# The norm of a feed-forward input moved behind the expanding product, onto GpSimd

## The chip, the cores and the metric

The kernel runs on one core of a Trainium2 chip, as one launch. The metric is the device time of that launch in microseconds (us). A core has a matrix engine (TensorE, in the rows PE, with its weight loads as PEld), two elementwise engines (VectorE, DVE, and ScalarE, ACT), a third, slower one (GpSimd, POOL) and a queue that issues DMAs (SyncE, SP). Each engine takes its instructions in order, and semaphores make one wait for another. Matrix products land in PSUM, which has eight banks of 128 x 512 numbers here; all else lives in SBUF.

## The reference

Two transformer blocks over 256 tokens of 2048 numbers. The first (two layers with three kinds of attention) and the mixer and memory attention of the second are not touched. The change lies in the last part of the second block:

```
h = rmsnorm(x, pre_norm_ffn)             # x * rsqrt(mean(x*x) + eps) * gain, per token
hid = h @ w_up                           # 2048 -> 2 * 5632
hid = causal convolution of width 3 over the tokens, per column, + bias
gate, up = split(hid)
x = x + rmsnorm((gelu(gate) * up) @ w_down, post_norm_ffn)
```

The norm factor rsqrt(...) is one number per token. It can be multiplied into h, or after the product into each row (token) of hid, but ahead of the convolution, which mixes tokens.

## The kernel before, in words

All products are done in split form: a 32-bit number is written as hi + lo, hi rounded to the matrix engine's format, and hi*hi + hi*lo + lo*hi are added up. Each 128 x 512 piece of a weight (**raw**) is brought in by a DMA from the SP queue (two pieces each, three buffers); ACT makes its **hi** by a copy (L431), DVE its **lo** by a subtraction raw - hi (L432). There are four hi and four lo buffers, so the split can run at most a few pieces ahead of the product that reads them.

The last part is `ffn`. Its input X (8 tiles, 2 x 128 tokens by 4 x 512 columns) is made by `close` of the attention before it: DVE and POOL add the attention's result to X (L1592, L1590), ACT sums the squares of the new X (L1597), DVE adds them up (L1601). `normT` then builds the transposed, normed, split input in 8 units of two 128-column pieces. For one unit, `unit` transposes four 128 x 128 tiles of X on PE into a PSUM bank (L566, tile trs, two banks), multiplies on DVE by the gain (a column vector) and the row of norms rb (L576), copies to hi on ACT (L583) and subtracts on DVE (L584). The row rb comes from the sums: DVE scales them (L409), POOL takes the power -1/2 (L410), two small PE products spread the two columns of 128 norms over all partitions (L599, tile rbt), and DVE copies that to SBUF (L607). Unit 0 cannot be scaled before rb is there.

The expanding product is 22 **blocks** of `denseT2`. A block makes four 128 x 256 results (two gate and two up column groups), each in its own PSUM bank (tiles upd, upd and ups, ups or upt, upo in turn), over 16 steps of 128 input columns (kt 0 to 15). A step takes one hi and one lo weight piece and does eight products (L539: weight hi by [h hi, h lo], 512 columns; L540: weight lo by h hi, 256 columns). Then `evac` empties the four banks. For each result: ACT copies the half with h lo to a tile **us** (L2012), DVE adds the other half from PSUM (L2013), ACT multiplies by the last convolution tap and adds the bias, into cv (L2014), and DVE adds the two shifted taps (L2015, L2017). After these come the gelu on ACT (L2019), the product gate * up on DVE (L2020) and the split of the result (L431, L432). The next block's products run on PE at the same time, into other banks, and its weight splits stand between these instructions on ACT and DVE. Three buffers serve the us tiles.

The order of the instructions on each engine is set by a scheduler from the code; it interleaves the evacuation of one block with the weight splits of the next. The contracting product (`dense`, w_down) follows, and at the end `post` with `close` adds the normed result to X and writes it out. `post` also fetches four rows of gains by DMAs from the POOL queue (L1557) for the contraction's evacuation.

Of the kernel before, what the change touches and what calls it, by code (L numbers as in the profile page):

```python
# [13 lines left out]
OP = mybir.AluOpType  # L14
# [4 lines left out]
D = 2048  # L19
# [1530 lines left out]
class Block2(Block1):  # L1550
# [447 lines left out]

    def ffn(self, X, ss, out):
        nc, a = self.nc, self.a  # L2000
        h = self.normT(X, self.gain("pre_ffn"), ss=ss, both=True)
        units = []
        for b in range(22):
            def evac(banks):
                c = {}
                for g in range(2):
                    c[g] = self.B("cv", bufs=4)
                    for i in range(2):
                        ct = g * 44 + 2 * b + i
                        p, d = banks[2 * g + i], c[g][:, i * 256:i * 256 + 256]  # L2010
                        s = self.temp("us")[:, :256]
                        nc.scalar.activation(s, p[:, 256:], AF.Copy)  # L2012
                        nc.vector.tensor_add(s, s, p[:, :256])  # L2013
                        nc.scalar.activation(d, s, AF.Identity, scale=self.v("cw2", ct), bias=self.v("cb", ct))  # L2014
                        nc.vector.scalar_tensor_tensor(d[:, 1:], s[:, :255], self.v("cw1", ct), d[:, 1:],  # L2015
                                                       op0=OP.mult, op1=OP.add)
                        nc.vector.scalar_tensor_tensor(d[:, 2:], s[:, :254], self.v("cw0", ct), d[:, 2:],  # L2017
                                                       op0=OP.mult, op1=OP.add)
                nc.scalar.activation(c[0], c[0], AF.Gelu_apprx_tanh)  # L2019
                nc.vector.tensor_mul(c[0], c[0], c[1])  # L2020
                new = (lambda name, dt: self.B(name, tag="act", bufs=16, dt=dt)) if b < 8 else None
                units.append(self.halves(c[0], new))

            self.denseT2(h, self.w("ffn_w_up_2"), [(256 * b, 256), (DFF + 256 * b, 256)], evac,
                         "ddss" if b % 2 else "ddto", what="up")
        ev, close = self.post(X, 2 * D, out)
        act = Act(256, 44, units.__getitem__)
        for j in range(4):
            self.dense(act, list(range(44)), self.w("ffn_w_down_2"), [(512 * j, 512)], [0, 1], ev(j), what="down")
        close()  # L2030
# [76 lines left out]
```

## Time and profile before

| | us |
|---|---|
| three timed runs | 3441.53, 3451.6, 3455.27 (median 3451.6) |
| the profiled execution | 3443.87, of which the span shown is 3442.1 |
| last product of the attention before | starts at 2678.57 |
| first expanding product | 2693.77 |
| last expanding product | 3184.1 |
| end of the span | 3442.1 |

The profile is one execution. Times in its rows count from the start of the span. A row of a timeline gives start, duration, engine, line, operation, output <- inputs with shapes, how many were merged into it, and in brackets how long the engine had been idle before it and what ended that. The names of tiles are those of the program without buffer numbers.

### The profile page before, as it was taken

How to read it: one execution, taken by the hardware profiler on the slowest of the kernel's cores; microseconds unless marked ns; L12 is line 12 of the kernel's file. 1: busy time of each engine (PE TensorE's matmuls, PEld its weight loads, DVE VectorE, ACT ScalarE, POOL GpSimd, SP SyncE). 2: the span in 40 equal slices, each digit the busy share in tenths (PEclk: the TensorE clock that was granted, in tenths of full speed). 3: DMA queues.
4: the chain of work that ended last, by engine and by line, in shares of the span. 5: the costliest groups of instructions: out<-in, count | busy, mean ns of one | idle time of the engine just before them, and what ended most of it. 6: DMA issues, size and time to landing. Idle time of an engine off the chain costs nothing. (4 is left out here: it accounts for less than half of the span.)

```text
span 3442.1 us, 51876 instructions
## 1 busy us (share of the span) xinstructions
PE 3323.3 (97%) x18122; PEld 2790.0 (81%) x18122; DVE 2335.5 (68%) x5073; ACT 1818.0 (53%) x3652; POOL 320.9 (9%) x472
## 2 busy tenths in 40 slices
PE   7999999999999999998999999999999899999998
PEld 4577778788788888887777999888788788888886
DVE  3478988778867575877674556555666777777554
ACT  3345655336435355765574445555555666666544
POOL 1022221103120121111110000000000000000000
PEclk9999999999999999999999999999999999999999
DMA  8845444642565544444454636666655466666665
GB/s 291 290 124 158 132 148 133 220 127 81 169 212 171 162 118 139 144 152 149 156 163 147 184 120 183 192 189 191 208 175 168 150 187 190 191 195 199 193 191 165
DMA packets 226758, 590.11 MB, mean 171 GB/s; under 512 B 39904, under 2 KB 63184, under 8 KB 226496
## 3 DMA queue, kind: packets, MB, share of 16 engines
q1 hardware_dynamic: 221104, 570.41, 53.5%
q0 software_dynamic: 4864, 15.69, 1.5%
q8 instruction: 142, 2.33, 0.3%
q14 instruction: 120, 0.98, 0.1%
q10 hardware_dynamic: 528, 0.71, 0.1%
HBM read 582.48 MB, written 4.24 MB: 170 GB/s over the span
## 5 line engine op out<-in xcount | busy, mean ns | idle before, releaser
L432 DVE TENSOR_TENSOR lo<-raw,hi 128x512 fp32r<-128x512 f32 (+3 forms) x1788 | 1200.3, 678 | 793.5 <-ACT hi L431 765.0
L431 ACT ACTIVATE hi<-raw 128x512 fp32r<-128x512 f32 (+3 forms) x1788 | 1086.9, 614 | 1180.0 <-DVE lo L432 324.2
L784 DVE SCALAR_TENSOR_TENSOR scr<-raw,cb 128x512 f32<-128x512 f32 x448 | 301.2, 698 | 31.2 <-DMA raw<-in_w_ada_dram 16.3
L410 POOL TENSOR_TENSOR sm<-sm,mhalf 128x2 f32<-128x2 f32 (+4 forms) x116 | 119.3, 1030 | 1383.8 <-DVE sm L409 1378.6
L492 PE MATMUL downd<-hi,hi 128*128 128x512 f32 x352 | 137.8, 391 | 0.0
L494 PE MATMUL downd<-hi,lo 128*128 128x512 f32 x352 | 137.7, 391 | 0.0
L493 PE MATMUL downd<-lo,hi 128*128 128x512 f32 x352 | 137.7, 391 | 0.0
L647 ACT ACTIVATE P<-Ss,sm 128x512 f32<-128x512 f32 (+1 forms) x164 | 99.4, 607 | 67.5 <-DVE sm L643 49.3
L539 PE MATMUL upd<-hi,hi 128*128 128x512 f32 x352 | 132.8, 394 | 0.0
L539 PE MATMUL upd<-lo,hi 128*128 128x512 f32 x352 | 132.1, 392 | 0.0
L419 ACT ACTIVATE PT<-pTt 128x256 f32<-128x256 f32 x226 | 79.2, 381 | 64.6 <-PE pTt L664 55.2
L492 PE MATMUL L0outd<-hi,hi 128*128 128x512 f32 x256 | 101.4, 396 | 4.3 <-DVE ot L1407 3.0
L516 PE MATMUL L0zd<-hi,lo 128*128 128x512 f32 x256 | 100.2, 392 | 2.2 <-DVE lo L432 2.1
L513 PE MATMUL L0zd<-hi,hi 128*128 128x512 f32 x256 | 100.6, 393 | 0.4 <-DVE kpe L425 0.4
L643 DVE TENSOR_REDUCE sm<-Ss 128x1 f32<-128x512 f32 (+1 forms) x164 | 95.0, 584 | 7.8 <-PE Ss L636 6.8
L494 PE MATMUL L0outd<-hi,lo 128*128 128x512 f32 x256 | 99.9, 392 | 0.3 <-DVE lo L432 0.3
L493 PE MATMUL L0outd<-lo,hi 128*128 128x512 f32 x256 | 100.1, 391 | 0.0
L515 PE MATMUL L0zd<-lo,hi 128*128 128x512 f32 x256 | 99.9, 390 | 0.0
L879 POOL CAST pad<-q 64x128 fp32r<-64x128 f32 x156 | 62.4, 407 | 401.4 <-PE Ss L636 313.0
L540 PE MATMUL upd<-hi,lo 128*128 128x256 f32 x352 | 98.9, 281 | 0.0
L540 PE MATMUL upd<-lo,lo 128*128 128x256 f32 x352 | 98.6, 281 | 0.0
L664 PE MATMUL pTt<-ident,P 128*128 128x128 f32 x536 | 87.3, 276 | 5.8 <-DVE PT L425 1.8
(616 smaller groups left out, 9374.1 us busy)
## 6 DMA issues: line engine op xcount, KB each, us to landing
raw<-in_w_in_dram SPq DMA_DIRECT2D x344, 512.0 KB, 3.7
raw<-in_w_ada_dram SPq DMA_DIRECT2D x384, 256.0 KB, 3.5
raw<-in_ffn_w_up_dram SPq DMA_DIRECT2D x176, 512.0 KB, 4.2
raw<-in_w_out_dram SPq DMA_DIRECT2D x104, 512.0 KB, 3.6
raw<-in_ffn_w_down_dram SPq DMA_DIRECT2D x88, 512.0 KB, 4.1
raw<-in_w_proj_b_dram SPq DMA_DIRECT2D x32, 512.0 KB, 4.1
raw<-in_w_in_dram SPq DMA_DIRECT2D x32, 288.0 KB, 3.3
raw<-in_w_proj_a_dram SPq DMA_DIRECT2D x16, 512.0 KB, 4.2
```

What stands on the lines that cost most here:

```text
L410: nc.gpsimd.tensor_tensor(r, ms, self.mhalf[:, :n], op=OP.pow)
L431: self.nc.scalar.activation(hi, src, AF.Copy)
L432: self.nc.vector.tensor_sub(lo, src, hi.bitcast(F32))
L492: nc.tensor.matmul(ps[t][:, a], lhsT=xh, rhs=hi[:, a], start=first, stop=False)
L493: nc.tensor.matmul(ps[t][:, a], lhsT=xh, rhs=lo[:, a], start=False, stop=False)
L494: nc.tensor.matmul(ps[t][:, a], lhsT=xl, rhs=hi[:, a], start=False, stop=last)
L513: nc.tensor.matmul(p, lhsT=hi[:, s], rhs=xh, start=kt == 0 and c % per == 0, stop=False, skip_group_check=True)
L515: nc.tensor.matmul(p, lhsT=hi[:, s], rhs=xl, start=False, stop=False, skip_group_check=True)
L516: nc.tensor.matmul(p, lhsT=lo[:, s], rhs=xh, start=False, stop=kt == nk - 1, skip_group_check=True)
L539: nc.tensor.matmul(banks[c], lhsT=hi[:, s], rhs=x, start=kt == 0, stop=False, skip_group_check=True)
L540: nc.tensor.matmul(banks[c][:, :256], lhsT=lo[:, s], rhs=x[:, :256], start=False, stop=kt == nk - 1, skip_group_check=True)
L784: nc.vector.scalar_tensor_tensor(self.temp("scr"), raw, 1.0, st[s], op0=OP.mult, op1=OP.mult, accum_out=st["p"][:, s, k, q:q + 1])
```

## The change

The units of the feed-forward input are made with `plain=True`: transposed, multiplied by the gain and split, without the row of norms. The first two units are asked for ahead of the norm's own instructions (`h.need(1)`). The row rb of norms is made once, into a tile of its own, and in `evac` POOL multiplies each us tile by it, between the addition of the two halves and the convolution.

```diff
     def ffn(self, X, ss, out):
         nc, a = self.nc, self.a
-        h = self.normT(X, self.gain("pre_ffn"), ss=ss, both=True)
+        h = self.normT(X, self.gain("pre_ffn"), both=True, plain=True)
+        h.need(1)
+        rb = self.rows([self.rstd(ss[t], 1, D) for t in range(2)], self.B("rb", bufs=1, cols=256))
         units = []
...
                         s = self.temp("us")[:, :256]
                         nc.scalar.activation(s, p[:, 256:], AF.Copy)
                         nc.vector.tensor_add(s, s, p[:, :256])
+                        nc.gpsimd.tensor_tensor(s, s, rb, op=OP.mult)
                         nc.scalar.activation(d, s, AF.Identity, scale=self.v("cw2", ct), bias=self.v("cb", ct))
```

With `plain=True`, `unit` takes its branch without rb (L574, a multiplication by the gain alone, in place of L576). Below `evac`'s new line the line numbers are three higher than before: the copy is L2014, the addition L2015, the new multiplication L2016, the tap and bias L2017, the shifted taps L2018 and L2020, the gelu L2022.

**PE where the feed-forward begins.** trs are the transposes of the units (28456 and 28468 units 0 and 1; 28533 and 28573 units 2 and 3), rbt the spread norms, upd the first expanding product. Before:

```order
L566 MATMUL trs_28491<-ident,x_4618_18303 128x128
L599 MATMUL rbt_28475<-ident,sm_28467 128x128
L599 MATMUL rbt_28475<-ident,sm_28471 128x128
L566 MATMUL trs_28533<-ident,x_4674_18516 128x128
L566 MATMUL trs_28533<-ident,x_4678_18524 128x128
```

Now:

```order
L566 MATMUL trs_28533<-ident,x_4678_18524 128x128
L566 MATMUL trs_28573<-ident,x_4674_18516 128x128
L599 MATMUL rbt_28489<-ident,sm_28481 128x128
L599 MATMUL rbt_28489<-ident,sm_28485 128x128
L539 MATMUL upd_28493<-hi_28464,hi_28381 128x512
L540 MATMUL upd_28493<-hi_28464,lo_28382 128x256
```

The spreading of the norms moved behind the transposes of units 2 and 3, and now stands directly ahead of the first expanding product.

**ACT at the evacuation of a block in the middle** (block 8 before, block 8 now; hi<-raw are the weight splits of the next block, cv the tap and bias). Before:

```order
L2012 ACTIVATE us_30990<-upd_30777 128x256
L2012 ACTIVATE us_30996<-upd_30778 128x256
L2014 ACTIVATE cv_30989<-us_30990,vt 128x256
L2012 ACTIVATE us_31003<-ups_30779 128x256
L2014 ACTIVATE cv_30989<-us_30996,vt 128x256
L431 ACTIVATE hi_31027<-raw_31025 128x512
L2014 ACTIVATE cv_31002<-us_31003,vt 128x256
L2012 ACTIVATE us_31009<-ups_30780 128x256
L431 ACTIVATE hi_31039<-raw_31025 128x512
L2019 ACTIVATE cv_30989<-cv_30989 128x512
```

Now:

```order
L2014 ACTIVATE us_31026<-upd_30813 128x256
L2014 ACTIVATE us_31033<-upd_30814 128x256
L2017 ACTIVATE cv_31025<-us_31026,vt 128x256
L2014 ACTIVATE us_31041<-ups_30815 128x256
L2017 ACTIVATE cv_31025<-us_31033,vt 128x256
L431 ACTIVATE hi_31067<-raw_31065 128x512
L431 ACTIVATE hi_31079<-raw_31065 128x512
L2017 ACTIVATE cv_31040<-us_31041,vt 128x256
L2014 ACTIVATE us_31048<-ups_30816 128x256
L431 ACTIVATE hi_31093<-raw_31091 128x512
L2022 ACTIVATE cv_31025<-cv_31025 128x512
```

One weight split moved ahead of the third tap; the first two splits still stand behind the first two taps, and each tap now waits for POOL's multiplication of its us tile.

**DVE at the same place** (lo<-raw are the weight splits). Before:

```order
L2013 TENSOR_TENSOR us_30990<-us_30990,upd_30777 128x256
L2013 TENSOR_TENSOR us_30996<-us_30996,upd_30778 128x256
L2015 SCALAR_TENSOR_TENSOR cv_30989<-us_30990,vt,cv_30989 128x255
L2013 TENSOR_TENSOR us_31003<-us_31003,ups_30779 128x256
L2017 SCALAR_TENSOR_TENSOR cv_30989<-us_30990,vt,cv_30989 128x254
L2015 SCALAR_TENSOR_TENSOR cv_30989<-us_30996,vt,cv_30989 128x255
L432 TENSOR_TENSOR lo_31028<-raw_31025,hi_31027 128x512
L2017 SCALAR_TENSOR_TENSOR cv_30989<-us_30996,vt,cv_30989 128x254
L2015 SCALAR_TENSOR_TENSOR cv_31002<-us_31003,vt,cv_31002 128x255
L2013 TENSOR_TENSOR us_31009<-us_31009,ups_30780 128x256
L2017 SCALAR_TENSOR_TENSOR cv_31002<-us_31003,vt,cv_31002 128x254
L432 TENSOR_TENSOR lo_31040<-raw_31025,hi_31039 128x512
```

Now:

```order
L2015 TENSOR_TENSOR us_31026<-us_31026,upd_30813 128x256
L2015 TENSOR_TENSOR us_31033<-us_31033,upd_30814 128x256
L2018 SCALAR_TENSOR_TENSOR cv_31025<-us_31026,vt,cv_31025 128x255
L2015 TENSOR_TENSOR us_31041<-us_31041,ups_30815 128x256
L2020 SCALAR_TENSOR_TENSOR cv_31025<-us_31026,vt,cv_31025 128x254
L2018 SCALAR_TENSOR_TENSOR cv_31025<-us_31033,vt,cv_31025 128x255
L432 TENSOR_TENSOR lo_31068<-raw_31065,hi_31067 128x512
L2020 SCALAR_TENSOR_TENSOR cv_31025<-us_31033,vt,cv_31025 128x254
L2018 SCALAR_TENSOR_TENSOR cv_31040<-us_31041,vt,cv_31040 128x255
L2015 TENSOR_TENSOR us_31048<-us_31048,ups_30816 128x256
L2020 SCALAR_TENSOR_TENSOR cv_31040<-us_31041,vt,cv_31040 128x254
L432 TENSOR_TENSOR lo_31080<-raw_31065,hi_31079 128x512
```

The first twelve stand as before. The next weight split is moved ahead of the fourth result's first shifted tap. POOL's queue, which had nothing between the norm's powers and the four DMAs of L1557, now holds 88 multiplications there, four for each block.

## Rows read from the trace of the kernel before

**Rows 1.** The page's first line.
```profile
span 3442.1 us, 51876 instructions
```

**Rows 2.** Busy time by stage: stretch, length, busy us (instructions) of each engine, TensorE's granted clock, DMA share, GB/s.
```profile
2678.00:2696.00 18.00, 7.85 (x31) 6.08 (x30) 14.43 (x31) 11.11 (x30) 6.03 (x6) 0.62 0.22 72
2696.00:3184.50 488.50, 488.50 (x2822) 430.14 (x2821) 358.26 (x666) 308.88 (x573) 2.19 (x4) 1.00 0.62 190
3184.50:3442.00 257.50, 243.11 (x1064) 199.25 (x1062) 136.05 (x206) 119.99 (x201) 4.94 (x4) 0.98 0.60 183
```

**Rows 3.** Waits from 2725 to 3180: total us, times, longest us.
```profile
PEld upd L540 <- DVE lo L432: 0.8, 3, 0.4
```

**Rows 4.** Timeline of PE where the feed-forward begins.
```profile
2689.56 1.31 PE L599 MATMUL rbt<-ident,sm 128*128 128x128 f32 x4 [4.79 <-POOL sm L410]
...
2693.77 0.78 PE L539 MATMUL upd<-hi,hi 128*128 128x512 f32 x1
...
2697.66 0.39 PE L539 MATMUL upd<-hi,hi 128*128 128x512 f32 x1
```

**Rows 5.** Timelines of ACT, POOL and DVE at the same place.
```profile
2687.92 0.61 ACT L1597 ACTIVATE sq<-x 128x512 f32<-128x512 f32 x1
...
2688.96 1.06 POOL L410 TENSOR_TENSOR sm<-sm,mhalf 128x1 f32<-128x1 f32 x2 [2.31 <-DVE sm L409]
...
2691.36 1.66 DVE L576 SCALAR_TENSOR_TENSOR h<-trs,vt,rb 128x256 f32<-128x256 f32 x4
...
2692.94 0.42 DVE L584 TENSOR_TENSOR hi<-h,hi 128x256 fp32r<-128x256 f32 x1
```

**Rows 6.** Timeline of ACT at the evacuation of block 8.
```profile
2894.94 0.39 ACT L2012 ACTIVATE us<-upd 128x256 f32<-128x256 f32 x1 [0.18 <-PE upd L540]
...
2895.91 0.59 ACT L2014 ACTIVATE cv<-us,vt 128x256 f32<-128x256 f32 x1
```

**Rows 7.** Timeline of DVE at the same evacuation.
```profile
2895.40 0.41 DVE L2013 TENSOR_TENSOR us<-us,upd 128x256 f32<-128x256 f32 x1
...
2900.17 0.68 DVE L432 TENSOR_TENSOR lo<-raw,hi 128x512 fp32r<-128x512 f32 x1
```

**Rows 8.** Timeline of weight loads, first use of the lo piece of kt 3.
```profile
2900.98 0.19 PEld L540 LDWEIGHTS upd<-lo,lo 128*128 128x128 f32 x1
```

**Rows 9.** Line L1129: duration ns min/median/max, first and last start.
```profile
L1129 POOL TENSOR_TENSOR H<-H,cs x32: 722/738/1192, 142.9 to 1277.9; 128x256 f32<-128x256 f32 x32
```

**Rows 10.** Timelines of POOL and DVE where both work on SBUF tiles.
```profile
176.49 0.77 POOL L1129 TENSOR_TENSOR H<-H,cs 128x256 f32<-128x256 f32 x1 [0.60 <-DMA H<-in_rp_dram]
...
176.59 1.23 DVE L432 TENSOR_TENSOR lo<-raw,hi 128x512 fp32r<-128x512 f32 x1
...
928.19 1.29 POOL L1410 TENSOR_TENSOR x<-xo,ot 128x512 f32<-128x512 f32 x1
...
928.62 1.42 DVE L432 TENSOR_TENSOR lo<-raw,hi 128x512 fp32r<-128x512 f32 x1 [0.75 <-ACT hi L431]
```

**Rows 11.** Timeline of PE after single idle stretches.
```profile
495.48 0.50 PE L493 MATMUL L0cqd<-lo,hi 128*128 128x512 f32 x1 [2.19 <-DVE lo L432]
495.82 0.39 PE L494 MATMUL L0cqd<-hi,lo 128*128 128x512 f32 x1
...
2576.85 0.58 PE L516 MATMUL xkd<-hi,lo 128*128 128x256 f32 x1 [3.12 <-DVE lo L432]
2577.23 0.41 PE L513 MATMUL xkd<-hi,hi 128*128 128x256 f32 x1
...
2579.99 0.28 PE L513 MATMUL xkd<-hi,hi 128*128 128x256 f32 x1
```

**Rows 12.** POOL's DMAs of gains, their landing, and DVE's first use of one.
```profile
3171.84 0.54 POOL L1557 DMA_DIRECT2D row<-in_vb_dram  x1 [0.85 <-PE ups L540]
...
row<-in_vb_dram POOLq DMA_DIRECT2D x4, 256.0 KB, 6.5
...
3245.71 0.69 DVE L1575 TENSOR_TENSOR y<-downd,row 128x512 f32<-128x512 f32 x1 [0.72 <-ACT sq L1573]
```

## The prediction

> **What bounds the kernel now.** I read the page's first line for the span, the table of busy time by stage, the waits inside the expanding product, and then timelines, engine by engine, at two places: where the feed-forward begins, and at one evacuation in the middle.
>
> The span is 3442.1 us [rows 1]. In the stretch of the expanding product, 488.5 us long, PE is busy for all 488.50 at a granted clock of 1.00, which is 2.4 GHz, while DVE works 358 us, ACT 309 and POOL 2 [rows 2]. So this stage is bound by PE; no change on another engine can shorten it, and POOL looks free. But the average hides how close DVE is. The one wait of PE's weight loads in it is on the weight split's lo: 0.8 us in three cases [rows 3]. Block 8 shows why: the lo piece of kt 3 is finished by DVE at 2900.17 + 0.68 = 2900.85 [rows 7], and its first weight load starts at 2900.98 [rows 8]. 0.13 us is all the cover there. The next block's fourth split stands on DVE behind nearly all of the evacuation, and the block is 488.5 / 22 = 22.2 us long, so what the evacuation is late by beyond 0.13 us PE loses 22 times.
>
> Where the feed-forward begins the chain is serial: in the 18 us from 2678 PE is busy for 7.85 at a mean clock of 0.62 [rows 2]. The last squares end at 2687.92 + 0.61 = 2688.53, the two powers on POOL run from 2688.96 to 2690.02 [rows 5], the spread norms end at 2689.56 + 1.31 = 2690.87, and the first expanding product starts at 2693.77 [rows 4].
>
> **Part 1: the beginning.** What stood between 2690.87 and 2693.77, 2.90 us, was the copy of rb, the multiplication of the first units (1.66 for four, from 2691.36), their copies on ACT and their subtractions on DVE (0.42 each, from 2692.94) [rows 5]. Now the transposes, the gain and the split need only X, and can be done ahead of the norms or beside them. But the spread norms stand on PE directly ahead of the first product, as the order shows, so PE still waits for the sums and the powers: the wait isn't removed, only what followed it. DVE does the four multiplications by the gain (1.66) and a subtraction (0.42) among the sums, and the second power has to wait for part of them. I put that at a quarter of their 2.08 us, 0.5, with a little for the product's own start: gain 2.90 - 0.6 = 2.3 us. Bounds: nothing (the norms become later by as much as is taken from behind them), and all 2.90. The multiplication by the gain in later units stays one instruction on DVE of about the same length: 0.
>
> **Part 2: 88 multiplications on POOL, four for each of 22 blocks.** Their own work is cheap: 128x256 of two SBUF inputs takes POOL 738 ns in the median, 722 to 1192 [rows 9], so 88 x 0.74 = 65 us in a stage of 488 in which POOL is idle. What counts is what they hold up, in two ways.
>
> First, the tap on ACT waits for POOL. In block 8 the first addition ends at 2895.40 + 0.41 = 2895.81 [rows 7] and the tap follows at 2895.91 [rows 6], a handoff of 0.10. Now the multiplication runs from 2895.91 to 2896.65 and the tap starts at 2896.75: 0.84 later. ACT is in order, and behind the first two taps stand the splits hi of the next block's kt 2 and kt 3; on DVE behind their shifted taps stand the two lo.
>
> Second, POOL and DVE do not run side by side on SBUF tiles. A split on DVE of 0.68 alone [rows 7] that was issued 0.10 behind the start of a POOL addition of 0.77 took 1.23, and one issued 0.43 behind the start of one of 1.29 took 1.42 [rows 10]. In both it ended about half a microsecond after POOL did (177.82 against 177.26; 930.04 against 929.48): it waited for POOL to end. So each multiplication costs DVE its whole length wherever DVE has a two-input SBUF instruction to do. The shifted taps and lo splits are of that kind.
>
> The sum to the lo of kt 3. The first multiplication delays everything behind it by 0.84. The second runs while ACT does the first tap (0.59) and DVE has nothing but that to wait for: 0. The third falls between the shifted taps of the first two results, the fourth directly ahead of the split of kt 3 (it follows the fourth addition, and the order on DVE has one shifted tap between that and the split): 0.74 each. Late by 0.84 + 0.74 + 0.74 = 2.32, less the cover of 0.13: 2.19 us of idle PE per block. The order also moved one hi split ahead of the third tap, which helps its ACT half, but the lo on DVE keeps its place, so I give no credit. Times 22 (the last block's evacuation lies beside the first steps of the contraction, which takes splits at nearly the same rate): 48.2 us. Once PE has stopped, the later splits have caught up by the same amount, and each block starts afresh.
>
> Bounds for a block: if POOL and DVE did not hinder each other, 0.84 - 0.13 = 0.71 us, in all 15.6; if all four multiplications came in series at the longest seen, 0.20 + 4 x 1.19 - 0.13 = 4.8, in all 106. A gain is excluded, since PE was never idle there. I take 2.19, as the rows of the same shape are at the median length when nothing precedes them on DVE.
>
> **What is hidden.** The four DMAs of gains on POOL's queue now stand behind the last multiplication. Their last was issued at 3171.84 and such a one lands in 6.5 us; DVE first needs one at 3245.71 [rows 12]. Issued some 8 us behind the end of the expanding product (3184.5 [rows 2]) they land by about 3200, still 45 us early: 0. Without that cover they would cost what they are late by. The us tiles have three buffers and are held 0.8 us longer; the fourth copy needs the first one's buffer, whose shifted taps stand before it on DVE anyhow: 0.
>
> **Sum.** The profiled execution took 3443.87 with its 3442.1 of span. 3443.9 - 2.3 + 48.2 = 3489.8; I forecast 3490. The median of the three runs, 3451.6, lies 7.7 above the profiled execution and would give 3497; the range takes that in.
>
> **Rivals.**
> 1. Not slower: the evacuation hides the multiplications. It has the next block's 22 us to finish in, and a hi split was moved forward. Then POOL and DVE would have to take turns in DVE's pauses, so that kt 3's lo is late by no more than its cover; from 0.9 us per block (17 + 2.3, over 22) the kernel is measurably slower. Against it: 0.13 us of cover, and the 1.23 and 1.42 of [rows 10]. Time: 3443.9 - 2.3 + 0 to 15.6, so 3442 to 3457.
> 2. The clock falls at each stop. After one idle stretch of 2.19 inside a dense stage, TensorE went on at 0.50 and 0.39 per 512 columns, full speed; after one of 3.12, with transposes ahead of it, 256 columns took 0.41 in place of 0.28, at half clock, from 2576.85 until before 2579.99 [rows 11]. Were it so in every block, 3.1 us at half clock would lose about 1.4 more: 22 x 1.4 = 31, time 3521. My stops are of the first kind, near its length, and may come in two pieces. The Trainium skill (TensorE: Matmul & The Clock Gate, "A second HAM failure mode: psum-queue depth-cycling") tells of a kernel in which frequent short idle stretches between groups of products made the clock swing between its two levels; the 0.39 behind 2.19 of idle speaks against that for single stops, and no row here has them every 22 us.
> 3. The multiplications come in series, or POOL waits for DVE each time: the bound of 4.8 per block, 3443.9 - 2.3 + 106 = 3548.
>
> **How the numbers follow.** The forecast's mechanism with 1.2 to 3.5 us per block (3468 to 3519) 0.69; rival 1 0.17; rival 2 0.09; rival 3 0.05. Range 3453 to 3530: it takes in the upper part of rival 1 and most of rival 2, and leaves out the lower part of rival 1 and rival 3. A measurement of this kernel can tell about 0.5%, 17 us, from no change. The front alone cannot give 17 us, so faster 0.03; rival 1 is within, with the lower end of the forecast: same 0.16; slower 0.81.
>
> **What would show it.** In the changed profile the expanding product's stretch from first to last product should be 22 x 24.4 = 537 us, with PE's idle time before L540 or L539 put down to DVE's lo (L432), about 2 us in each block, all at kt 2 to kt 5; the clock in it at 1.00; the multiplications at 0.74 to 1.2 us; splits of 1.2 us and more beside those of 0.68; the first product 2 us sooner behind the last squares, directly behind rbt. If PE is without idle time there, rival 1 holds; if 256-column products at 0.41 follow the stops, rival 2; if the stops are near 0.7 with the splits at 0.68, the two engines do not hinder each other in these forms, and my sum is wrong by its second and third terms.

## The result

The changed kernel took 3476.8 us (median of four runs, 3473.4 to 3480.9), the kernel before 3452.2 beside it (four runs, 3441.5 to 3455.3): the ratio is 1.0076, with an interval of [1.0055, 1.0097]. It is slower by 0.8%, a difference clear of the spread of the runs: 24.5 us in the medians and 34.8 between the two profiled executions (3478.65 against 3443.87). The forecast was +45.9 on the profiled execution of before. So the direction was right and the main mechanism too; the size was a third too large against the profiled pair, and nearly twice the difference of the medians. Among the runs of the experiments, two executions at a granted clock of 0.58 and 0.71 (5543.7 us of the multiplication by ones, 4331.9 us of the changed kernel with deeper buffers) are left out of every comparison.

The page's first line and the busy time by stage, to set beside [rows 1, 2] (stretch, length, busy us of PE, PEld, DVE, ACT, POOL, granted clock, DMA share, GB/s):

```profile
span 3476.8 us, 51962 instructions
```
```profile
2680.60:2698.60 18.00, 9.54 (x34) 7.03 (x33) 14.23 (x31) 11.06 (x30) 6.69 (x6) 0.65 0.21 69
2696.80:3217.70 520.90, 510.63 (x2831) 433.28 (x2831) 368.44 (x667) 306.46 (x574) 94.93 (x86) 1.00 0.58 176
3217.70:3476.80 259.10, 243.03 (x1057) 197.91 (x1055) 135.85 (x204) 119.06 (x200) 10.41 (x11) 0.98 0.60 184
```

In the middle row PE is no longer busy throughout (510.63 of 520.90), at an unchanged clock of 1.00. The waits that took its place, from 2725 to 3200 (total us, times, longest), against the 0.8 us of [rows 3]:

```profile
ACT cv L2017 <- POOL us L2016: 46.0, 40, 1.7
DVE cv L2018 <- ACT cv L2017: 41.6, 40, 1.3
...
PEld upd L540 <- DVE lo L432: 27.1, 62, 0.8
...
PE upd L540 <- DVE lo L432: 9.8, 22, 0.5
```

Weight loads run ahead of the products, so not all of the 27.1 us reaches PE, and the ends of products are modelled. I therefore measure a stop by the distance from one product's start to the next, less the usual distance. The last expanding product of the kernel before starts at 3185.52; the 3184.1 of the table of times ahead of the prediction is the last one into a tile upd, 1.4 us sooner, and the expectations of the first experiments count the stretch to there (490.3 and 521.3 us for what are 491.75 and 522.76 here). They also count the way to the first expanding product from the end of the attention's last product, 0.4 us behind its start. With that, the 34.7 us by which the span grew divide so:

| part | before | after | difference |
|---|---|---|---|
| up to the attention's last product | 2678.57 | 2681.28 | +2.7 |
| from there to the first expanding product | 15.2 | 13.4 | -1.8 |
| first to last expanding product | 491.75 | 522.76 | +31.0 |
| of which block 0 (1.3 of it at half clock) | | | +1.6 |
| of which stops in blocks 1 to 21 | | | +23.6, 1.13 a block |
| of which a slower pace between the stops | | | +5.8, 0.27 a block |
| contraction and the rest (all of it stops in its first 17 us) | 256.6 | 259.4 | +2.8 |

The first line lies ahead of everything that was changed.

**The beginning.** PE's and POOL's timelines, to set beside [rows 4, 5] (start, duration, engine, line, operation, count, idle time before and what ended it):

```profile
2693.17 0.79 PE L599 MATMUL rbt<-ident,sm 128*128 128x128 f32 x2 [0.26 <-POOL sm L410]
2694.23 0.80 PE L599 MATMUL rbt<-ident,sm 128*128 128x128 f32 x2 [0.27 <-POOL sm L410]
2694.68 0.78 PE L539 MATMUL upd<-hi,hi 128*128 128x512 f32 x1
...
2696.11 0.63 PE L539 MATMUL upd<-hi,hi 128*128 128x512 f32 x1
...
2699.31 0.59 PE L539 MATMUL upo<-lo,hi 128*128 128x512 f32 x1
...
2699.86 0.39 PE L539 MATMUL upd<-hi,hi 128*128 128x512 f32 x1
```
```profile
2692.45 1.73 POOL L410 TENSOR_TENSOR sm<-sm,mhalf 128x1 f32<-128x1 f32 x2 [3.09 <-DVE sm L409]
```

The granted clock stands directly behind the five engines' busy times. First the kernel before, then the changed one:

```profile
2695.00:2696.00 1.00, 1.00 (x5) 0.90 (x4) 0.91 (x3) 0.60 (x2) 0.00 (x0) 0.50 0.00 0
2696.00:2697.00 1.00, 1.00 (x8) 0.87 (x7) 0.06 (x1) 0.00 (x0) 0.00 (x0) 0.99 0.00 0
```
```profile
2698.00:2699.00 1.00, 1.00 (x5) 0.90 (x4) 0.00 (x0) 0.00 (x0) 0.00 (x0) 0.50 0.00 0
2699.00:2700.00 1.00, 1.00 (x5) 0.81 (x4) 0.00 (x1) 0.67 (x2) 0.00 (x0) 0.63 0.00 0
```

The first expanding product now follows the spread norms at once, but these start 0.9 us later behind the attention than before (11.9 in place of 11.0), with a second power that ends later still: the gain and the splits now stand among the sums on DVE and ACT. It gained 1.8 us of the 2.90 that stood between. In this trace most of that is given back: the first products ran at 0.63 per 512 columns, at a granted clock of 0.50 (1.2 GHz, half clock), until about 2699.7. That is 5.0 us from the first product, where it had been 2.2 us before. Relative to the attention's end full clock came about 1 us later than before. The first sixteen products lost 1.3 us by it, and the transposes of a later unit ahead of kt 4, three in place of one, another 0.3.

The time at half clock isn't set by the new front alone. Seven traces (the changed kernel's and six of the experiments') have the first product 13.4 us behind the attention, and their first sixteen products took from 0.05 us (the first two results only) to 1.4 us longer than before.

**One block.** DVE, POOL, ACT and the weight loads at the evacuation of block 8, to set beside [rows 6 to 8]:

```profile
2909.35 0.41 DVE L2015 TENSOR_TENSOR us<-us,upd 128x256 f32<-128x256 f32 x1
...
2911.98 0.48 DVE L2020 SCALAR_TENSOR_TENSOR cv<-us,vt,cv 128x254 f32<-128x254 f32 x1
2912.38 0.97 DVE L2018 SCALAR_TENSOR_TENSOR cv<-us,vt,cv 128x255 f32<-128x255 f32 x1
2913.27 0.68 DVE L432 TENSOR_TENSOR lo<-raw,hi 128x512 fp32r<-128x512 f32 x1
...
2914.99 0.47 DVE L2020 SCALAR_TENSOR_TENSOR cv<-us,vt,cv 128x254 f32<-128x254 f32 x1
2915.38 1.28 DVE L432 TENSOR_TENSOR lo<-raw,hi 128x512 fp32r<-128x512 f32 x2
```
```profile
2909.85 1.43 POOL L2016 TENSOR_TENSOR us<-us,rb 128x256 f32<-128x256 f32 x2 [16.24 <-DVE us L2015]
2912.14 0.92 POOL L2016 TENSOR_TENSOR us<-us,rb 128x256 f32<-128x256 f32 x1 [0.86 <-DVE us L2015]
2915.14 2.12 POOL L2016 TENSOR_TENSOR us<-us,rb 128x256 f32<-128x256 f32 x1 [2.08 <-DVE us L2015]
```
```profile
2908.91 0.38 ACT L2014 ACTIVATE us<-upd 128x256 f32<-128x256 f32 x1 [0.19 <-PE upd L540]
...
2910.62 0.60 ACT L2017 ACTIVATE cv<-us,vt 128x256 f32<-128x256 f32 x1 [0.62 <-POOL us L2016]
...
2917.30 0.60 ACT L2017 ACTIVATE cv<-us,vt 128x256 f32<-128x256 f32 x1 [1.71 <-POOL us L2016]
```
```profile
2914.00 0.19 PEld L540 LDWEIGHTS upd<-hi,lo 128*128 128x128 f32 x1 [0.27 <-DVE lo L432]
...
2916.11 0.19 PEld L540 LDWEIGHTS upd<-lo,lo 128*128 128x128 f32 x1 [0.76 <-DVE lo L432]
...
2919.07 0.19 PEld L540 LDWEIGHTS upd<-lo,lo 128*128 128x128 f32 x1 [0.22 <-DVE lo L432]
```

The first product with the lo of kt 3, before and now:

```profile
2901.21 0.28 PE L540 MATMUL upd<-lo,lo 128*128 128x256 f32 x1
```
```profile
2916.11 0.39 PE L540 MATMUL upd<-lo,lo 128*128 128x256 f32 x1 [0.44 <-DVE lo L432]
```

Count from the first copy to us (2908.91 here, 2894.94 before). The first tap starts at 1.71 in place of 0.97: 0.74 later, for POOL's multiplication between the addition and it. The third multiplication was issued at 2912.14, beside a shifted tap of 0.48 that wasn't disturbed; the next shifted tap took 0.97, 0.50 longer. So the split of kt 3 starts at 6.47 in place of 5.23, late by 0.74 + 0.50 = 1.24. What PE lost by it up to kt 3 is 0.97 us a block (mean of blocks 2 to 20: 0.26 at kt 2, 0.71 at kt 3). That is 0.27 less than the lateness, and not only the 0.13 that stood between the split's end and its weight load: the load was issued ahead of need, and the product itself started at 2901.21, 0.36 behind the split's end at 2900.85. The fourth multiplication was issued at 2915.14, 0.24 ahead of that split. It did not hold the split up. It took 2.12 us itself and ended at 2917.26, 0.6 behind the end of two splits (2915.38 + 1.28 = 2916.66): POOL waited for DVE. What that cost is a late fourth tap and, through it, a late split for kt 5: the weight load at 2919.07 waited 0.22, and PE lost 0.15 us a block there. The 0.97 and the 0.15 make up the 1.13 of the table.

The lengths fall into these few values in every block: 0.74, 0.74, 0.92 and 2.12 for the four multiplications, 0.97 for one shifted tap and about 0.48 for the others.

```profile
L2016 POOL TENSOR_TENSOR us<-us,rb x88: 733/826/2122, 2720.7 to 3221.9; 128x256 f32<-128x256 f32 x88
```

**The contraction's start.** POOL, ACT and PE, and the DMAs issued from 3225 to 3231 (KB each, median us to landing):

```profile
3223.95 2.18 POOL L1557 DMA_DIRECT2D row<-in_vb_dram  x4
```
```profile
3233.06 2.43 ACT L431 ACTIVATE hi<-raw 128x512 fp32r<-128x512 f32 x4 [4.00 <-DMA raw<-in_ffn_w_down_dram]
```
```profile
3233.74 0.51 PE L492 MATMUL downd<-hi,hi 128*128 128x512 f32 x1 [0.91 <-ACT hi L431]
```
```profile
raw<-in_ffn_w_down_dram SPq DMA_DIRECT2D x3, 512.0 KB, 6.3
row<-in_vb_dram POOLq DMA_DIRECT2D x3, 256.0 KB, 5.9
```

In the kernel before, from 3192 to 3200:

```profile
raw<-in_ffn_w_down_dram SPq DMA_DIRECT2D x3, 512.0 KB, 4.5
```

Of the 2.8 us, 1.1 are stops beside the evacuation of the last block, of the kind seen in every block. The other 1.7 stand 15 to 17 us into the contraction, where ACT waited 4.0 us for a weight piece. The four DMAs of gains, which now follow the last multiplication, were in flight beside the pieces of w_down, which took 6.3 us to land where such pieces took 4.5 in the kernel before. In every trace with the gains issued 4 to 8 us behind the last expanding product and the usual buffers (this one, the ones again, the fill, the last two results, no wait) PE stops there for 0.9 to 2.0 us. Where they were issued earlier, or 0.5 us behind it (the first two results), it does not. That the gains are the cause fits these traces; no run tested it alone.

### The profile page after: what moved, and what is told of

Same layout as the page of the kernel before. It is cut to its first block, busy times and chain, and to the rows that moved or that the text cites. A ratio compares the mean times of both kernels' runs of the same rounds, so it can differ in the third digit from the quotient of the medians.

```text
span 3476.8 us, 51962 instructions
## 1 busy us (share of the span) xinstructions
PE 3348.3 (96%) x18122; PEld 2795.9 (80%) x18122; DVE 2343.1 (67%) x5073; ACT 1814.4 (52%) x3652; POOL 419.8 (12%) x560
## 5 line engine op out<-in xcount | busy, mean ns | idle before, releaser
L2016 POOL TENSOR_TENSOR us<-us,rb 128x256 f32<-128x256 f32 x88 | 98.3, 1127 | 431.6 <-DVE us L2015 431.6
```

## The experiments

The theory called A in the expectations is the forecast's, with the fourth multiplication put right: the taps wait for POOL, POOL and DVE exclude one another on SBUF tiles, and PE pays what exceeds the cover. The expectations were written in three batches: first the front alone, the multiplication alone, the exclusion without the wait and the deeper buffers; then the halves, the control of the deeper buffers and the multiplication on DVE; last the fill and the multiplication by ones once more. Each could use only what the batches ahead of it had shown. Stops and pace are given for a block, as the mean of blocks 1 to 21.

**The front alone.** Changed kernel without its multiplication; the norm is left out of the result.

```diff
-                        nc.gpsimd.tensor_tensor(s, s, rb, op=OP.mult)
```

> The changed kernel without the multiplication on GpSimd: it leaves the norm out of the feed-forward, so only the moved beginning is left. Theory A (the whole loss comes from the 88 multiplications, by the tap's wait and by DVE and POOL excluding each other on SBUF tiles): the stretch from the first to the last expanding product is as before, 490.3 us (the changed kernel has 521.3), PE without idle time in it, and the first product 1.6 us sooner behind the end of the attention's last product than before (13.2 us in place of 14.8): time about 3450, within 0.2% of before. Rival (the new order of transposes and norms at the beginning, or the gain alone in place of gain times norm, costs something): stretch over 495 or time over 3458.

Measured: 3444.0 us, ratio 0.9986 [0.9971, 1.0001] with ten runs. The first product came 13.4 us behind the attention, as in the changed kernel; the stretch was 493.3 us, 1.5 more than before: 0.9 at half clock and 0.3 of transposes in block 0, and 0.3 in the last block. No stop came in between. So the front costs nothing that shows and gives at most what the interval allows, 0.3% (the trace has 1.8 us sooner and 1.5 given back). The loss comes with the multiplications.

**The multiplication alone.** Kernel before, with POOL multiplying by a row of ones.

```diff
         h = self.normT(X, self.gain("pre_ffn"), ss=ss, both=True)
+        rb = self.B("rb", bufs=1, cols=256)
+        nc.vector.memset(rb, 1.0)
...
+                        nc.gpsimd.tensor_tensor(s, s, rb, op=OP.mult)
```

> The kernel before, with its normed input, and in addition the multiplication on GpSimd of every us tile by a tile of ones: the multiplication alone. Theory A: the same order of instructions in the blocks as in the changed kernel and the same loss, 1.41 us of idle PE per block, so the stretch is 521 us and the time 3452 + 31 = 3483, some 2 us above the changed kernel and a little more with the contraction's first steps. Rival (the changed kernel's loss comes from the beginning or from the values of the unnormed input): 3452.

Measured: 3477.8 to 3481.6 in three runs, ratio 1.0091 [1.0069, 1.0114]. The time was as expected. The trace is that of one further run of the same kernel.

> The kernel of e2 (normed input and a multiplication by ones) once more, for its trace: theory A: the multiplications at 0.74, 0.74, 0.92 and 2.12 us in each block, one shifted tap at 0.96, stops of 1.1 us per block in blocks 1 to 21, stretch 519 to 523. Rival (the loss in e2 lies elsewhere): stretch under 500.

Measured: one run of 3475.3; first product 15.2 us behind the attention as before, stretch 521.5, stops 1.15, pace 0.3 slower. The multiplications:

```profile
L2016 POOL TENSOR_TENSOR us<-us,rb x88: 733/827/2125, 2716.5 to 3218.1; 128x256 f32<-128x256 f32 x88
```

The same lengths as in the changed kernel, to the hundredth of a microsecond: the loss belongs to the multiplication and not to the new order of the front.

**The lock without the wait.** Changed kernel; POOL writes its product into a tile that nobody reads, so the taps don't wait for it. The norm is left out of the result.

```diff
+        idle = self.B("idle", bufs=1, cols=256)
...
-                        nc.gpsimd.tensor_tensor(s, s, rb, op=OP.mult)
+                        nc.gpsimd.tensor_tensor(idle, s, rb, op=OP.mult)
```

> The changed kernel with GpSimd's product written to a tile that nobody reads, so that it reads the us tile and rb as before but no tap waits for it (the norm is left out of the result). The multiplications stay, the wait goes. Theory A, in which the two engines exclude each other: 1.24 us of lateness at the split of kt 3 was 0.74 from the tap's wait and 0.50 from one shifted tap held up; without the wait the multiplications meet other instructions of DVE, hold up one to three of them by 0.1 to 0.7 each, and PE loses 0.3 to 1.0 us per block: stretch 497 to 512, time 3457 to 3472; some DVE instructions last 0.8 to 1.2 us in place of 0.48 or 0.68. Rival B (only the tap's wait costs; the lengthened instruction lies in a pause): stretch 490, time 3450. Rival C (only the exclusion costs, the wait is absorbed): 521, 3477.

Measured: 3464.1 us, ratio 1.0047 [1.0028, 1.0066]; stretch 508.6, stops 0.56, pace 0.2.

```profile
L2017 POOL TENSOR_TENSOR idle<-us,rb x88: 735/843/1451, 2727.8 to 3214.7; 128x256 f32<-128x256 f32 x88
...
L2019 DVE SCALAR_TENSOR_TENSOR cv<-us,vt,cv x88: 469/486/965, 2728.5 to 3215.5; 128x255 f32<-128x255 f32 x88
```

Nobody waits for POOL's result, and still PE stops. Ahead of the split of kt 2 one shifted tap took 0.96 in place of 0.48 and one 0.64: 0.64 in all. PE lost 0.46 up to kt 3 and 0.07 at kt 4, on the mean of blocks 2 to 20. ACT's copies did not wait for a us buffer held by POOL in this trace, so that rival falls. The exclusion alone carries about half of the stops, though at other meetings of POOL and DVE than in the changed kernel.

**POOL at work without reading.** Changed kernel; a fill takes the place of the multiplication, at the same place and with the same waits. The values of the feed-forward are left out.

```diff
-                        nc.gpsimd.tensor_tensor(s, s, rb, op=OP.mult)
+                        nc.gpsimd.memset(s, 0.01)
```

> The changed kernel with GpSimd's multiplication of each us tile replaced by filling that tile with a constant (the feed-forward's values are left out): the same order of instructions in the blocks and the same waits of the taps, but GpSimd reads nothing from SBUF and is done sooner, some 0.3 us by the 0.204 of a fill of half the size. Theory A (the exclusion is between two readers of SBUF): the first tap is 0.3 late in place of 0.74; no fill lasts longer than the first, no shifted tap longer than 0.48; the stop per block is 0.3 less 0.13, about 0.2 us, the split of kt 5 is on time: stretch 495 to 503, time 3453 to 3460. Rival (any work of GpSimd on SBUF excludes DVE): the fourth fill waits out DVE's run of splits again and lasts about 1.7 us in place of 0.3, the second result's first shifted tap is lengthened by 0.2 or more, and a stop stands at kt 5.

Measured: 3451.8 us, ratio 1.0013 [0.9999, 1.0026]; stretch 497.1, stops 0.13. The time is slightly below what was expected, the stretch within it. POOL's fills and DVE's shifted taps:

```profile
L2016 POOL MEMSET us<- x88: 312/313/318, 2727.8 to 3202.3; 128x256 f32 x88
...
L2018 DVE SCALAR_TENSOR_TENSOR cv<-us,vt,cv x88: 471/477/484, 2728.8 to 3203.8; 128x255 f32<-128x255 f32 x88
```

Neither engine is ever held up: no tap of this line took more than 0.484, no fill more than 0.318. The third and the fourth fill of block 8 lay beside a running shifted tap for 0.31 us and took no longer than the first. With the reading the hold-up is gone. The Trainium skill (SBUF — State Buffer, "Who interferes with whom") states this rule: a DVE instruction with two SBUF inputs contends with a GpSimd instruction that reads SBUF, not with one that only writes. The trace agrees (0.313 and 0.484 here against 2.12 and 0.97). A shorter POOL instruction, 0.31 against 0.74, is changed with it, so the small stops don't separate wait and length.

**Halves.** Changed kernel, multiplication for the first two results of a block only (the other two left without the norm), and for the last two only (g == 1 in place of g == 0).

```diff
-                        nc.gpsimd.tensor_tensor(s, s, rb, op=OP.mult)
+                        if g == 0:
+                            nc.gpsimd.tensor_tensor(s, s, rb, op=OP.mult)
```

> The changed kernel with the multiplication on GpSimd only for the first two of a block's four results (the up half goes without the norm). Theory A: the first tap is 0.74 late and with it the splits, nothing holds up DVE further: 0.74 less the cover of 0.13 is 0.6 us of stop per block (the changed kernel has 1.13 in blocks 1 to 21), and the products run at the slower pace seen behind stops, 0.27 more: stretch 508 to 513, time 3464 to 3470. If the exclusion alone counted (B): first two meet no DVE instruction in the changed trace, so no stop: stretch 492, time 3449. The shares of e4 and e5 should add up to the changed kernel's 1.13.

Measured: 3461.5 us, ratio 1.0023 [1.0010, 1.0036]; stretch 506.9, stops 0.51, pace 0.2. The stretch is 1 us or a little more below what was expected, the time 2.5.

```profile
L2017 POOL TENSOR_TENSOR us<-us,rb x44: 737/741/745, 2722.3 to 3204.3; 128x256 f32<-128x256 f32 x44
...
L2019 DVE SCALAR_TENSOR_TENSOR cv<-us,vt,cv x88: 468/477/486, 2723.7 to 3209.3; 128x255 f32<-128x255 f32 x88
```

No shifted tap of this line is lengthened. This half is the pure wait: the tap is 0.74 late and PE stops for 0.51, all of it at kt 3, where 0.74 less 0.13 would have been 0.61.

> The changed kernel with the multiplication only for the last two of a block's four results (the gate half goes without the norm). Theory A: the first taps are on time; the third multiplication holds up one shifted tap by 0.5, less 0.13 is 0.37 of stop, and the fourth, which loses to DVE, delays the fourth tap and with it the split of kt 5 a little: 0.4 to 0.6 us per block, with the slower pace 0.7 to 0.9: stretch 507 to 512, time 3462 to 3469; third multiplication 0.9 us, one shifted tap of the second result near 0.96. If only the taps' wait counted (B), the wait falls on the third tap, behind which no early split stands now: no stop, stretch 492, time 3449.

Measured: 3463.3 us, ratio 1.0033 [1.0020, 1.0045]; stretch 508.4, stops 0.41, pace 0.3: as expected.

```profile
L2017 POOL TENSOR_TENSOR us<-us,rb x44: 911/1220/2127, 2721.2 to 3205.6; 128x256 f32<-128x256 f32 x44
```

Only the lengths 0.92 and 2.12 are left, but for one of 1.52 in block 0. This half is the exclusion. Its stops divide into 0.21 at kt 3, where 0.50 less 0.13 would have been 0.37, and 0.15 at kt 5 from the fourth multiplication (mean of blocks 2 to 20; the 0.41 has a longer stop in block 1). Up to kt 3 the two halves make 0.51 + 0.21 = 0.72 of the whole's 0.97. The missing 0.25 is the cover, which each half used up for itself: as PE's products see it, the cover is 0.23 to 0.29 in these three kernels.

**The multiplication on DVE.**

```diff
-                        nc.gpsimd.tensor_tensor(s, s, rb, op=OP.mult)
+                        nc.vector.tensor_tensor(s, s, rb, op=OP.mult)
```

> The changed kernel with the multiplication by the row of norms on DVE in place of GpSimd (tensor times tensor, 128x256, some 0.34 us of DVE's time each). No handoff and no exclusion, but four more instructions, and the order puts all four ahead of the first split of the next block: counted from the start of the first addition ten more instructions of 0.34 to 0.40 us stand ahead of it than the two before, so the split of kt 2 ends 6.2 us behind the first copy where PE wants it at 4.65: 1.5 us of stop per block, with the slower pace 1.8: stretch 528 to 534, time 3483 to 3492. If GpSimd's handoffs and the exclusion are what costs, and DVE's order doesn't: stretch under 510, time under 3467.

Measured: 3476.7 us, ratio 1.0066 [1.0042, 1.0091]; stretch 519.7. The stop is 1.46, as expected, but 0.2 of it comes back in shorter distances directly behind it. The pace between stops is the usual one in 17 of 21 blocks, not the slower one that was expected, and so the time came out below.

```profile
L2016 DVE TENSOR_TENSOR us<-us,rb x88: 414/423/428, 2723.3 to 3221.7; 128x256 f32<-128x256 f32 x88
```
```profile
PEld upd L540 <- DVE lo L432: 28.7, 23, 1.4
```

At 0.42 a multiplication, DVE does in 88 x 0.42 = 37 us what POOL spends 95 us on, and the kernel's time is no different within the intervals. Moving the work to the idle POOL gained nothing here.

**More cover.** Changed kernel with a fifth hi and lo buffer (every fifth pair goes to tiles of their own) and three pieces split ahead in place of two (deep is 3 in the feed-forward); and, as its control, the same on the kernel before.

```diff
-        if self.loaded and len(self.whole) < 2:
+        if self.loaded and len(self.whole) < self.deep:
...
+            self.fifth += self.deep - 2
+            if self.fifth % 5 == 4:
+                hi, lo = (self.B(x, tag="w" + x, bufs=1, dt=F32R) for x in ("hi", "lo"))
```

> The changed kernel with a fifth pair of buffers for the split weights in the feed-forward, so that the split may run three pieces ahead in place of two; nothing else. If the loss is lateness beyond the cover of kt 3's lo (0.13 us before), one more step of 1.39 us covers the 1.24: the stops vanish or fall under 0.3 us per block, stretch 490 to 497, time 3446 to 3458. Rival (DVE or ACT as a whole can't keep up once POOL takes its share, so that lateness would carry on from block to block): stretch about 521 and time about 3477 as in the changed kernel.

Measured: 3456.0 us in nine runs, ratio 1.0024 [1.0013, 1.0035]; stretch 501.8. The time is within what was expected, the stretch above it. Stops fell to 0.18 a block, 3.8 us in all, with POOL's lengths unchanged (0.74, 0.74, 0.92, 2.12). So the price of a multiplication is what its lateness exceeds the cover by. What kept the stretch up is the pace, +5.3 us.

> The kernel before with the fifth pair of buffers for split weights, the control for e6. In the kernel before no split is late, so more cover gives nothing: stretch 490 to 492 with 2.77 us for each pair of steps, time 3449, within 0.2%. If the 5 us that e6 still had (2.82 us for a pair without a stop) come from the fifth buffers, this kernel has them too: stretch 497, time 3454. If they come with GpSimd's work, it has not.

Measured: 3453.4 us, ratio 1.0001 [0.9984, 1.0018]; stretch 497.7, 5.9 more than before: not one stop, 5.3 of it pace in blocks 1 to 21 and 0.6 in block 0. The busy time over as long a stretch as that of [rows 2], 488.5 us:

```profile
2696.00:3184.50 488.50, 488.50 (x2790) 426.12 (x2789) 356.39 (x659) 304.26 (x566) 2.19 (x4) 1.00 0.60 188
```

PE is busy throughout at clock 1.00 in both, but starts 2790 products here against 2822 there: 175.1 ns for one in place of 173.1. POOL multiplies nothing here, so the slower pace of the deep kernels comes with the fifth buffers and the third piece split ahead that they allow. The deep buffers take away 20 of the 24 us of stops of the changed kernel and leave the pace where it was there. No version beats the kernel before by what a measurement can tell; the front alone comes nearest.

## Why the prediction was right, and where its size was off

- **The binding resource and the path** were right: PE's loads wait for DVE's lo at kt 2, kt 3 and kt 5, in every block, and POOL's multiplications make it late. The kernel with deeper buffers shows that the cover decides. The cover itself was read too small: 0.13 is right for the weight load, but PE's products lost 0.27 less than the lateness.
- **First multiplication, 0.84 late**: 0.74. POOL started 0.09 behind the addition (2909.76, 2909.85), as assumed, and the first of the two multiplications in 1.43 takes 0.735; but the tap followed that by 0.04 in place of the 0.10 assumed.
- **Third multiplication, 0.74**: 0.50. It was issued beside a running tap and the next one waited only for the rest of it. [Rows 10] already spoke against "its whole length": the two splits took 1.23 and 1.42 in place of 0.68, longer by 0.55 and 0.74 behind POOL instructions of 0.77 and 1.29.
- **Fourth multiplication, 0.74 "directly ahead of the split of kt 3"**: 0. This is the term that failed. [Rows 10] had only cases in which POOL was first and DVE waited, and the sum took that for the rule. Here DVE went first, twice in a row, and POOL waited; its lateness fell on the fourth tap, which has time, and returned only as 0.15 at kt 5. Forecast 2.19 a block, measured 1.13.
- **The size is partly luck.** The multiplications were forecast at 48.2 us; their stops measured 23.6 in 21 blocks and 1.1 beside the contraction's start, 24.7 together, half of it. The total came nearer because things without a term were added: the slower pace (5.8), the stop behind the DMAs of gains (1.7) and 2.7 ahead of the change.
- **Beginning, 2.3 sooner**: 1.8. What the sum did not have is the clock: in this trace the first products ran at a granted clock of 0.50 for 5.0 us in place of 2.2 and lost 1.3. The front alone is worth about 0.3 us in its trace, 1.8 less 1.5; in the traces with the same front the loss at half clock varies from 0.05 to 1.4.
- **DMAs of gains, priced at 0**: the rows were read rightly, since they land long before DVE needs them. The sum asked only whether they are late themselves, not what they are in flight beside; the weight pieces beside them were late, and a stop of 1.7 stands there.
- **Not foreseen**: the slower pace, +5.8 us, for which the sum had neither a term nor a bound.
- **The rivals.** The clock stayed at 1.00 through 21 blocks of stops, with 0.39 per 512 columns between, so the second fell. The first (hidden) needed cover that this kernel doesn't have; with a fifth buffer it comes nearly true, at 3456. The third's series didn't come about, though single multiplications of 2.12 exceed the 1.19 that bounded it.
- **The remaining 2.7 us** of the profiled difference lie ahead of the change, and the medians, 24.5 apart, are closer than the profiled pair. Part of the 34.8 is therefore spread between executions of one kernel: that of before varied by 14 us.

## What to carry to other kernels

Price an instruction inserted into a chain by the cover of the first thing behind it that the bound engine needs, not by the helper engine's idle share: here, with about a quarter of a microsecond of cover, four multiplications of 0.74 us on an idle engine cost 1.1 us a block. When POOL and DVE both read SBUF, as here, work out for each meeting which of them waits, because the loser's followers pay; where it can't be told, both are the bounds. A start that came 1.8 us sooner out of an idle stretch was worth less than its lead, by an amount that differed between traces of one front, because the clock had still to rise. And when instructions go into a queue, ask which DMAs they push back, and what those will then be in flight beside.

## What the runs showed of the hardware that was not expected

- **Who waits was the same at each place in every block.** In all 22 blocks the third multiplication went ahead of a shifted tap that stood ready on DVE, and the fourth, issued 0.24 us ahead of a split, waited out that and another one. The Trainium skill (SBUF — State Buffer, "Who interferes with whom") says that the order of issue decides; these starts, as the profile records them, don't show it for the fourth. It was issued while a shifted tap (2914.99 to 2915.46) was running, as was the third (2911.98 to 2912.46); why one won against the next DVE instruction and the other lost against two isn't settled.
- **Two paces at full clock.** With all 16 products of two steps back to back and the clock at 1.00, a pair of steps takes 2.77 or 2.82 us. I count the blocks, of blocks 1 to 21, in which at least three of the eight pairs are slow. There is none before or with the front alone; there are 14 in the changed kernel, 4 to 18 in the other kernels with POOL at work, 4 with the multiplication on DVE, whose stops are longer, and all 21 with the fifth buffers, with stops or without. The median length of one product as the trace has it, before, after, with the fifth buffers on the kernel before and with DVE:

```profile
L539 PE MATMUL upd<-hi,hi x352: 390/391/775, 2693.8 to 3183.5; 128*128 128x512 f32 x176
```
```profile
L539 PE MATMUL upd<-hi,hi x352: 388/396/775, 2694.7 to 3215.4; 128*128 128x512 f32 x176
```
```profile
L544 PE MATMUL upd<-hi,hi x352: 391/396/775, 2693.0 to 3188.6; 128*128 128x512 f32 x176
```
```profile
L539 PE MATMUL upd<-hi,hi x352: 387/392/774, 2697.8 to 3215.6; 128*128 128x512 f32 x176
```

  The 391 or 392 ns go with the usual pace, the 396 with the slower one. Its cause stays open; it accounts for 5.8 of the 34.8 us.
- **These short stops didn't cost the clock.** 21 blocks of 23.4 to 24.0 us, most with three stops each of 0.15 to 0.7 us, left the granted clock at 1.00.
